# Chunk order of the last product pair, and where a norm adds its epsilon

## The chip, the cores and the metric

The kernel runs on one core of one Trainium2 chip. The metric is the device time of one execution in microseconds. The core has a matrix engine (TensorE, PE in the profile), three engines for elementwise work (VectorE, DVE; ScalarE, ACT; GpSimd, POOL) and SyncE (SP), which here only issues DMAs. GpSimd issues DMAs as well.

## The reference

Two layers of a hybrid of linear attention and chunked softmax attention, on 512 tokens of width 2048, in float32. Cut to what matters here:

```python
def hybrid_layer(x, ...):
    h = rmsnorm(x, g_pre)
    z = h @ w_in                       # one projection, split by columns
    gq, gk, gv, gg, ga, aq, ak, av, ag = split_columns(z)
    ...
    o_gla = gla_chunk_causal(...)      # 4 heads, value width 256
    o_gla = rmsnorm(o_gla, g_gla.reshape(GLA_HEADS, GLA_DV)).reshape(B, S, D_GLA)
    o_gla = o_gla * jax.nn.silu(gg)
    o_att = ...                        # 8 heads of softmax attention, normed and gated
    y = jnp.concatenate([o_gla, o_att], axis=-1) @ w_out
    return x + rmsnorm(y, g_post)
```

with `rmsnorm(x, g) = x * rsqrt(mean(x*x) + EPS) * g`, EPS = 1e-6.

## The kernel before

**Weights.** Each weight matrix is cut into blocks of 512 columns, and each block into eight pieces of 256 rows (512 KB each). A piece is a job in one long list, `stream`. A job is loaded by a DMA on SyncE into a ring of four tiles (`raw` or `H`), then split in two parts: ScalarE rounds it (`wh`, line 195), VectorE subtracts the rounded from the full (`wl`, line 199). TensorE multiplies three times: high by high, high by low, low by high. A loop keeps loads up to five jobs ahead of the products. When VectorE has read a `raw` tile for its low part, the tile is free for a later load.

**Pairs.** Most blocks are taken two at a time by `fast_gemm`, which multiplies a 2 by 2 arrangement of sub-matrices with seven products (P1 to P7) in place of eight. Each product runs over four chunks c = 0 to 3 of the inner dimension. The list `PROD` (for the last pair of a layer, `PROD_END`) gives the order of (product, chunk). The products P5, P6, P3 and P7 take sums of activation blocks as their operand (S1, S2, S4, S3). VectorE adds or subtracts the weight pieces for P5, P6, P7 and, in the last pair, P4 (lines 190 and 192). When a product's last chunk is done, its result is evacuated: P1, P5 and P6 by ScalarE copies, the others by VectorE (lines 357 to 361) and then a consumer, for the output projection `project` (square on ScalarE, line 1214, times a gain on VectorE, line 1217).

**The sums of the last pair.** The activations of the output projection are the gated heads. `output_sums` loads their four parts for a chunk (SyncE, lines 623 and 627, tiles `t`, from `fa` and `fg`), makes S1, S3, S2, S4 in turn on VectorE (lines 603 to 612), splits each (lines 108 and 109), and stores it to DRAM from GpSimd's queue (line 597, tensors `oS`). A job of P5 then loads its S1 back into a ring of four tiles named `sa` (line 180). The sums of chunks 2 and 3 (the attention heads 4 to 7 with the linear heads 2 and 3) are made while the value projection's products still run; those of chunks 0 and 1 only when all heads are done, during the block before the last pair. In program order a load of weights for P5 comes ahead of the load of its S1.

**The end of a layer.** Four blocks of the output projection: block 0 for all four token tiles, block 1 for the first two, the last pair (blocks 2 and 3, `W23`, with `end=True`), then block 1 for the other two token tiles. For the last block the attention operands of the second token half are loaded again by `fetch_last`, one with each chunk of P4, into `sa`. The table `OO` gives the order in which block 1 goes through its chunks.

**The linear heads.** A `Unit` is one head and one token half. Its steps: `outer` and `states` make the chunk states, `read` multiplies them with the queries (line 1071), `norm` squares the result on ScalarE with a sum along the row (line 1081, two calls), adds epsilon on VectorE (line 441, in `rms_scale`) and raises to the power of -0.5 on GpSimd (line 437); `gate` scales on VectorE (line 1089); `turn` transposes on TensorE (line 1099), evacuates on ScalarE (line 1110), splits, and stores to `fg`. There are four heads and two token halves, 8 units a layer and 16 in all. The operand tiles of the last two units are named `a` and `g` in the profile.

**Order.** All instructions are traced in the program's order, and the framework then plans each engine's order ahead of time on a simulated timeline (`schedule_with_timeline_sim=True`), so that an instruction which the plan thinks ready can go ahead of an earlier one that it thinks is waiting. On the chip the order of each engine and of each DMA queue is fixed.

Of the kernel before, what the change touches and what calls it, by code (L numbers as in the profile page):

```python
# [7 lines left out]
F32 = mybir.dt.float32  # L8
F32R = mybir.dt.float32r
BF16 = mybir.dt.bfloat16  # L10
AF = mybir.ActivationFunctionType
ALU = mybir.AluOpType
# [3 lines left out]
P = 128  # L16
# [9 lines left out]
EPS = 1e-6  # L26
# [8 lines left out]
def hybrid_trunk(  # L35
# [13 lines left out]
    nc = tc.nc  # L49
    cpool = ctx.enter_context(tc.tile_pool(name="cpool", bufs=1))  # L50
# [15 lines left out]
    def nm(s):  # L66
        serial[0] += 1
        return f"{s}_{serial[0]}"
# [10 lines left out]
    def ev():  # L79
        return tmp.tile([P, 512], F32, tag="ev", name=nm("ev"), bufs=6)  # L80
# [4 lines left out]
    def sm(cols, tag="sm", bufs=None):  # L85
        return small.tile([P, cols], F32, tag=tag, name=nm(tag), **({"bufs": bufs} if bufs else {}))

    def aux():
        return ps_ax.tile([P, 512], F32, tag="ax", name=nm("ax"))
# [30 lines left out]
    chunk_ind = cst[:, 2 * P : 2 * P + 2]  # L120
    ones = cst[:, 2 * P + 2 : 3 * P + 2]
    mhalf = cpool.tile([P, 4], F32, tag="mhalf", name="mhalf")
    later = cpool.tile([P, P], F32R, tag="later", name="later")

    CO = (0, 4, 1, 5, 2, 6, 3, 7)
    OO = (5, 4, 7, 6, 2, 3, 0, 1)
    PAIRS = ((GG0, GG1), (AV0, AV1), (QK01, QK23), (QK45, QK67), (GK, GQ), (GV0, GV1))
    W23 = (NB_IN + 2, NB_IN + 3)
    MIDDLE = [("P6", 0), ("P3", 0), ("P6", 1), ("P3", 1), ("P6", 2), ("P6", 3), ("P3", 2), ("P3", 3)]

    def products(*names):
        return [(p, c) for p in names for c in range(4)]

    PROD = products("P1", "P5") + MIDDLE + products("P7", "P2", "P4")
    PROD_END = products("P1", "P2", "P5") + MIDDLE + products("P7", "P4")
    LEFT = {"P5": "S1", "P6": "S2", "P3": "S4", "P7": "S3", "P4": "A22"}
    last_cast, last_load, last_low = [None], [None], [None]
    made = set()
# [68 lines left out]
    for l in range(L):  # L207
# [3 lines left out]
        for b0, b1 in PAIRS:  # L211
            pr = {}
            stream += [Job(l, k, c, b0, b1, pr) for k, c in PROD]
        for b in (NB_IN, NB_IN + 1):
            stream += [Job(l, "std", c, b) for c in OO]
        pr = {}
        stream += [Job(l, k, c, *W23, pr) for k, c in PROD_END]
        stream += [Job(l, "std", c, NB_IN + 1) for c in OO]
# [9 lines left out]
    def take(l, blk, kind, c):  # L228
        i = cursor[0]
        job = stream[i]  # L230
        assert (job.l, job.b0, job.kind, job.c) == (l, blk, kind, c)
        for what in ("load", "high", "low"):
            prepare(what, i + 1)
        cursor[0] += 1
        return job

    def ahead():
        i = cursor[0]
        for what, n in (("load", 3), ("high", 3), ("low", 3), ("load", 4), ("high", 4), ("load", 5)):
            prepare(what, i + n)  # L240
# [89 lines left out]
    def fast_gemm(l, pair, consume, rate=0.0, skip=0, feature_major=False, after=None, end=False, scaled=True):  # L330
        b0 = pair[0]
        acc = {n: [ps_mm.tile([P, W], F32, tag="mm", name=nm("mm")) for _ in range(2)] for n in roles[0]}
        roles.reverse()
        target = {"P1": "X", "P5": "Y", "P6": "X", "P3": "Y", "P7": "X", "P2": "Y", "P4": "X"}
        starts = ["P1", "P5", "P2"]
        if end:
            target.update(P2="Z", P4="Y")
            starts.append("P4")
        prod = PROD_END if end else PROD
        pace = Pace(rate, skip)  # L340
        keep = {}

        def copies(name, src):
            keep[name] = []
            for t in range(2):
                e = ev()
                if scaled:
                    nc.scalar.activation(e, src[t], AF.Copy, scale=inv_rms(l, 2 * (name == "p5") + t))
                else:
                    nc.scalar.copy(e, src[t])  # L350
                keep[name].append(e)

        def combine(ps, h, t, kept, sign, op):
            def f(dst):
                if scaled:
                    r = (inv_rms if sign > 0 else neg_inv_rms)(l, 2 * h + t)
                    nc.vector.scalar_tensor_tensor(out=dst, in0=ps, scalar=r, in1=kept, op0=ALU.mult, op1=op)
                elif sign > 0:
                    nc.vector.tensor_tensor(out=dst, in0=ps, in1=kept, op=op)
                else:  # L360
                    nc.vector.tensor_tensor(out=dst, in0=kept, in1=ps, op=ALU.subtract)
            return f

        def finished(k, t):
            x_, y_ = acc["X"][t], acc["Y"][t]
            if k == "P3":
                consume(1, 0, t, None, combine(y_, 0, t, keep["x"][t], 1, ALU.subtract))
            elif k == "P7":
                consume(1, 1, t, None, combine(x_, 1, t, keep["p5"][t], -1, ALU.add))
            elif k == "P2":  # L370
                consume(0, 0, t, None, combine(acc[target[k]][t], 0, t, keep["p1"][t], 1, ALU.add))
            elif k == "P4" and end:
                consume(0, 1, t, None, combine(y_, 1, t, keep["x"][t], 1, ALU.add))
            elif k == "P4":
                consume(0, 1, t, x_, None)

        def matmuls(job, k, c, ts):
            a = job.a if job.a is not None else A[{"P1": (0, 0, c), "P2": (1, 0, c), "P4": (1, 1, c)}[k]]
            out_ps = acc[target[k]]
            fresh = k in starts and c == 0  # L380
            for kk in range(2):
                if feature_major:
                    for ft in range(4):
                        f = slice(ft * P, (ft + 1) * P)
                        tok = slice(kk * 256, (kk + 1) * 256)
                        dst = out_ps[ft // 2][:, (ft % 2) * 256 : (ft % 2 + 1) * 256]
                        ops = ((job.wh, 0), (job.wh, 1), (job.wl, 0))
                        for m, (lhs, part) in enumerate(ops):
                            nc.tensor.matmul(  # L389
                                dst, lhs[:, kk, f], a[:, part, tok],  # L390
                                start=(fresh and kk == 0 and m == 0 and ft % 2 == 0),
                                stop=(c == 3 and kk == 1 and m == 2), skip_group_check=True,
                            )
                else:
                    for t in ts:
                        tok = slice(kk * 256 + t * P, kk * 256 + (t + 1) * P)
                        ops = ((0, job.wh), (0, job.wl), (1, job.wh))
                        for m, (part, rhs) in enumerate(ops):
                            nc.tensor.matmul(  # L399
                                out_ps[t], a[:, part, tok], rhs[:, kk, :],  # L400
                                start=(fresh and kk == 0 and m == 0),
                                stop=(c == 3 and kk == 1 and m == 2), skip_group_check=True,
                            )

        if end:
            acc["Z"] = None
        for k, c in prod:
            if k == "P2" and end and c == 0:
                acc["Z"] = [aux(), aux()]
            job = take(l, b0, k, c)  # L410
            matmuls(job, k, c, range(2))
            ahead()
            if c == 3:
                if k == "P1":
                    copies("p1", acc["X"])
                elif k == "P5":
                    copies("p5", acc["Y"])
                elif k == "P6":
                    copies("x", acc["X"])
                else:  # L420
                    for t in range(2):
                        finished(k, t)
                    if k == "P7" and end:
                        copies("x", acc["X"])
            if after is not None:
                after(k, c)
            pace()
# [10 lines left out]

    def rms_scale(out_r, ms):
        v = sm(ms.shape[-1])  # L440
        nc.vector.tensor_scalar(out=v, in0=ms, scalar1=EPS, scalar2=None, op0=ALU.add)
        rsqrt(out_r, v)

    def square_sum(out_ss, pieces):
# [53 lines left out]
    def inv_rms(l, t):  # L498
        return norm[l][:, 0, t : t + 1]
# [139 lines left out]
    for i in range(10):  # L639
        nc.tensor.matmul(ps_w, warm[:, 0:P], warm, start=True, stop=True)  # L640
    nc.gpsimd.memset(mhalf, -0.5)
    nc.vector.tensor_copy(later, cst[:, P : 2 * P])

    fg_weights = {}
# [27 lines left out]
    def layer(l):  # L672
# [106 lines left out]
        fresh = set()  # L779
# [496 lines left out]

        def fetch_last(k, c):
            if k == "P4":
                i = OO[c] - 4
                op_att[1, i] = rtile("sa", (2, 512), F32R)  # L1280
                nc.sync.dma_start(flat(op_att[1, i]), oa_d[l][1, i])

# [75 lines left out]
```

## Time and profile before

| what | us |
|---|---|
| three runs | 1666.9, 1667.8, 1672.28 (median 1667.8) |
| the profiled execution | 1665.86, its span 1664.1 |
| block 0, the linear heads and block 1 (636 to 726, layer 0): TensorE busy | 86.71 of 90 |
| P1, P2 and P5 of the last pair (726 to 756, layer 0) | 28.03 of 30 |
| the rest of the last pair (756 to 806, layer 0) | 49.88 of 50 |
| the same three in layer 1 (1462 to 1551, 1551 to 1584, 1584 to 1634) | 86.47 of 89, 29.09 of 33, 50.00 of 50 |
| the tail (1634 to 1664) | 21.71 of 30 |

A row of a timeline gives the start, the duration, the engine, the line, the operation, output<-input, shapes, how many instructions of that kind are merged into the row, and in brackets the idle time of the engine before it with what ended it. Rows of DMA instructions in a queue (SPq, POOL) show the time of the issue, not of the transfer. A row of the chain of waits gives start, duration and what the chain went through; there a DMA lasts from issue to landing. A row of a group (L..., xcount) ends with total busy us, mean ns of one, and idle time before them. A row of windows gives the stretch, its length, busy time of PE, PEld, DVE, ACT and POOL, the granted clock, the busy share of the DMA engines and GB/s. PE's matmuls overlap: one of 512 columns is shown as 0.39 us, but they start closer together.

### The profile page before, as it was taken

What the parts mean: (1) busy time and instruction counts of PE and PEld (TensorE: products, weight loads), DVE (VectorE), ACT (ScalarE), POOL (GpSimd) and SP (SyncE); (2) the same over time, 40 slices, a digit from 0 to 9 for tenths busy, and PEclk for the clock granted to TensorE, in tenths of its full rate; (3) what the DMA queues carried; (4) which work ended last, traced back from release to release, by engine and by line L of the source; (5) the groups of instructions that cost most, each with busy time, mean ns of one, the idle gap of its engine ahead of it and who ended that gap; (6) DMA issues with size and microseconds to landing.
All of it is one profiled execution on the core that took longest, in us unless ns stands there. A gap on an engine that the chain in (4) does not pass through costs nothing.

```text
span 1664.1 us, 24933 instructions
## 1 busy us (share of the span) xinstructions
PE 1634.7 (98%) x9030; PEld 1396.2 (84%) x9030; DVE 1226.4 (74%) x1595; ACT 901.4 (54%) x1499; POOL 166.5 (10%) x260
## 2 busy tenths in 40 slices
PE   9999999999999999999999999999999999999997
PEld 7888889999988877687888878899999888777776
DVE  7566776877876876678886676768778778856787
ACT  7444544565766544454784445445567665445443
POOL 1210000000100101310122000000010011013101
PEclk9999999999999999999999999999999999999999
DMA  9979786868867788798889687868587677878986
GB/s 378 343 269 321 282 305 232 301 188 301 280 193 271 276 322 265 272 337 302 292 290 399 221 331 258 312 224 297 193 312 249 223 275 287 298 240 302 347 291 234
DMA packets 150779, 470.64 MB, mean 283 GB/s; under 512 B 16428, under 2 KB 35636, under 8 KB 150656
## 3 DMA queue, kind: packets, MB, share of 16 engines
q1 hardware_dynamic: 127632, 389.36, 67.7%
q0 software_dynamic: 22304, 78.41, 12.3%
q8 instruction: 71, 1.16, 0.3%
q10 hardware_dynamic: 720, 1.28, 0.2%
q14 instruction: 52, 0.43, 0.1%
HBM read 396.88 MB, written 72.11 MB: 282 GB/s over the span
## 4 chain that ended last, share of the span: by engine, by line
PE 89%; DMA 6%; DVE 3%; issue 1%; ACT 1%; POOL 0%; DVEq 0%; SPq 0%; ACTq 0%; POOLq 0%
PE mm L399 41%; PE mm L314 19%; PE mm L389 18%; DMA raw<-in_w_dram 3%; PE ax L875 2%; DVE wl L199 1%; DMA t<-fg 1%; PE ax L858 1%; PE ax L1037 1%; PE ax L706 1%; DMA sa<-S 1%; PE ax L1071 1%; PE ax L836 1%; PE ax L838 1%; PE ax L837 1%
## 5 line engine op out<-in xcount | busy, mean ns | idle before, releaser
L399 PE MATMUL mm<-wh,sa 128*128 128x512 f32 x1536 | 487.7, 392 | 5.6 <-ACT wh L195 3.5
L195 ACT CAST wh<-raw 128x1024 fp32r<-128x1024 f32 x256 | 269.4, 1055 | 253.4 <-PE mm L399 84.7
L199 DVE TENSOR_TENSOR wl<-raw,wh 128x1024 fp32r<-128x1024 f32 x256 | 311.3, 1218 | 91.7 <-PE mm L314 30.9
L195 ACT CAST wh<-H 128x1024 fp32r<-128x1024 f32 x224 | 234.8, 1051 | 217.9 <-PE mm L399 122.3
L399 PEld LDWEIGHTS mm<-wh,sa 128*128 128x128 f32 x1536 | 288.6, 188 | 68.5 <-ACT wh L195 6.4
L199 DVE TENSOR_TENSOR wl<-H,wh 128x1024 fp32r<-128x1024 f32 x224 | 272.7, 1221 | 79.8 <-PE mm L399 29.8
L399 PE MATMUL mm<-wl,sa 128*128 128x512 f32 x768 | 301.5, 393 | 4.7 <-DVE wl L199 4.7
L389 PE MATMUL mm<-sa,wh 128*128 128x256 f32 x1280 | 238.1, 285 | 0.0
L389 PEld LDWEIGHTS mm<-sa,wh 128*128 128x128 f32 x1280 | 200.3, 191 | 0.5
L399 PE MATMUL mm<-wh,a 128*128 128x512 f32 x576 | 184.6, 392 | 0.0
L389 PE MATMUL mm<-sa,wl 128*128 128x256 f32 x640 | 181.3, 283 | 0.2 <-DVE wl L199 0.2
L399 PEld LDWEIGHTS mm<-wl,sa 128*128 128x128 f32 x768 | 144.6, 188 | 37.2 <-DVE wl L199 7.6
L314 PE MATMUL mm<-wh,a 128*128 128x512 f32 x512 | 172.3, 402 | 2.6 <-DVE g L1217 0.9
L190 DVE TENSOR_TENSOR H<-H,raw 128x1024 f32<-128x1024 f32 x120 | 145.7, 1220 | 11.2 <-DMA raw<-in_w_dram 9.5
L192 DVE TENSOR_TENSOR raw<-H,raw 128x1024 f32<-128x1024 f32 x56 | 68.6, 1225 | 82.4 <-DMA raw<-in_w_dram 82.2
L399 PEld LDWEIGHTS mm<-wh,a 128*128 128x128 f32 x576 | 108.0, 188 | 22.3
L437 POOL TENSOR_TENSOR sm<-sm,mhalf 128x4 f32<-128x4 f32 (+2 forms) x40 | 54.3, 1357 | 694.0 <-DVE sm L885 450.6
L389 PEld LDWEIGHTS mm<-sa,wl 128*128 128x128 f32 x640 | 122.4, 191 | 0.5 <-DVE wl L199 0.4
L314 PEld LDWEIGHTS mm<-wh,a 128*128 128x128 f32 x512 | 98.1, 192 | 26.1 <-DVE g L1217 1.8
L399 PE MATMUL mm<-wl,a 128*128 128x512 f32 x288 | 113.5, 394 | 0.0
L314 PE MATMUL mm<-wl,a 128*128 128x512 f32 x256 | 102.2, 399 | 0.0
L389 PE MATMUL mm<-a,wh 128*128 128x256 f32 x512 | 94.7, 284 | 0.0
(205 smaller groups left out, 2345.0 us busy)
## 6 DMA issues: line engine op xcount, KB each, us to landing
raw<-in_w_dram SPq DMA_DIRECT2D x320, 512.0 KB, 5.2
sa<-S SPq DMA_DIRECT2D x192, 512.0 KB, 4.8
H<-in_w_dram SPq DMA_DIRECT2D x56, 512.0 KB, 4.8
sa<-A SPq DMA_DIRECT2D x48, 512.0 KB, 5.5
S<-g POOLq DMA_DIRECT2D x32, 512.0 KB, 7.7
oS<-g POOLq DMA_DIRECT2D x32, 512.0 KB, 6.4
sa<-oS SPq DMA_DIRECT2D x32, 512.0 KB, 5.1
sg<-t POOLq DMA_DIRECT2D x32, 256.0 KB, 5.8
```

The source lines that it names most:

```text
L190: nc.vector.tensor_tensor(out=h, in0=h, in1=r, op=ALU.add)
L192: nc.vector.tensor_tensor(out=r, in0=h, in1=r, op=ALU.subtract)
L195: last_cast[0] = nc.scalar.copy(self.wh, src).ins
L199: last_low[0] = nc.vector.tensor_tensor(out=self.wl, in0=self.src, in1=self.wh.bitcast(F32), op=ALU.subtract).ins
L314: mm = nc.tensor.matmul(pss[o], a[:, part, t], rhs[:, kk, :], start=(i == 0 and kk == 0 and m == 0), stop=(i == n - 1 and kk == 1 and m == 2),
L389: nc.tensor.matmul(dst, lhs[:, kk, f], a[:, part, tok], start=(fresh and kk == 0 and m == 0 and ft % 2 == 0), stop=(c == 3 and kk == 1 and ...
L399: nc.tensor.matmul(out_ps[t], a[:, part, tok], rhs[:, kk, :], start=(fresh and kk == 0 and m == 0), stop=(c == 3 and kk == 1 and m == 2), ...
L437: nc.gpsimd.tensor_tensor(out=out_r, in0=v, in1=mhalf[:, : v.shape[-1]], op=ALU.pow)
L706: nc.tensor.matmul(ps[0:96, half * 256 : (half + 1) * 256], wga[kt // 10][:, kt % 10, :], op[:, i, (kt % 2) * 256 : (kt % 2 + 1) * 256], s ...
L836: nc.tensor.matmul(ps[:, :n], self.qh[:, t], self.kh[:, :n], start=True, stop=False)
L837: nc.tensor.matmul(ps[:, :n], self.qh[:, t], self.kl[:, :n], start=False, stop=False)
L875: nc.tensor.matmul(o, self.pt[i][:, j * P : (j + 1) * P], av[hd // 4, j // 2][:, j % 2, (hd % 4) * P : (hd % 4 + 1) * P], start=(j == 0), ...
```

## The change

Two parts. In the last pair of each layer every product takes its chunks in the order 2, 3, 0, 1: `C_END` replaces 0, 1, 2, 3 in `PROD_END`, the first and the last chunk of a product (which start and stop the accumulation, and set off the evacuation) follow it, and `fetch_last` looks its index up through it, so that the k-th chunk of P4 still fetches the k-th operand. In `rms_scale`, which only `norm` of the linear heads calls, the epsilon is added by ScalarE (Identity with a bias from a tile of one column, set once by GpSimd at the start) where VectorE added it.

```diff
+    eps = cpool.tile([P, 1], F32, tag="eps", name="eps")
...
-    MIDDLE = [("P6", 0), ("P3", 0), ("P6", 1), ("P3", 1), ("P6", 2), ("P6", 3), ("P3", 2), ("P3", 3)]
-
-    def products(*names):
-        return [(p, c) for p in names for c in range(4)]
-
-    PROD = products("P1", "P5") + MIDDLE + products("P7", "P2", "P4")
-    PROD_END = products("P1", "P2", "P5") + MIDDLE + products("P7", "P4")
+    C_IN, C_END = (0, 1, 2, 3), (2, 3, 0, 1)
+    MIDDLE = (("P6", 0), ("P3", 0), ("P6", 1), ("P3", 1), ("P6", 2), ("P6", 3), ("P3", 2), ("P3", 3))
+
+    def products(cs, *names):
+        return [(p, c) for p in names for c in cs]
+
+    def middle(cs):
+        return [(p, cs[i]) for p, i in MIDDLE]
+
+    PROD = products(C_IN, "P1", "P5") + middle(C_IN) + products(C_IN, "P7", "P2", "P4")
+    PROD_END = products(C_END, "P1", "P2", "P5")
+    PROD_END += middle(C_END) + products(C_END, "P7", "P4")
...
         prod = PROD_END if end else PROD
+        c_first, *_, c_last = C_END if end else C_IN
...
-            fresh = k in starts and c == 0
+            fresh = k in starts and c == c_first
...
-                                stop=(c == 3 and kk == 1 and m == 2), skip_group_check=True,
+                                stop=(c == c_last and kk == 1 and m == 2), skip_group_check=True,
...
-            if k == "P2" and end and c == 0:
+            if k == "P2" and end and c == c_first:
                 acc["Z"] = [aux(), aux()]
...
-            if c == 3:
+            if c == c_last:
...
     def rms_scale(out_r, ms):
         v = sm(ms.shape[-1])
-        nc.vector.tensor_scalar(out=v, in0=ms, scalar1=EPS, scalar2=None, op0=ALU.add)
+        nc.scalar.activation(v, ms, AF.Identity, bias=eps)
         rsqrt(out_r, v)
...
     nc.gpsimd.memset(mhalf, -0.5)
+    nc.gpsimd.memset(eps, EPS)
...
         def fetch_last(k, c):
             if k == "P4":
-                i = OO[c] - 4
+                i = OO[C_END.index(c)] - 4
```

More of the change, by code (lines that the diff above doesn't have):

```diff
@@ L401, in matmuls @@
                                 start=(fresh and kk == 0 and m == 0),
-                                stop=(c == 3 and kk == 1 and m == 2), skip_group_check=True,
+                                stop=(c == c_last and kk == 1 and m == 2), skip_group_check=True,
                             )
```

## The prediction

> **What bounds the kernel now.** I read the page first, then the list of waits of TensorE, then the timelines of the places that it names.
>
> ```profile
> span 1664.1 us, 24933 instructions
> ...
> PE 1634.7 (98%) x9030; PEld 1396.2 (84%) x9030; DVE 1226.4 (74%) x1595; ACT 901.4 (54%) x1499; POOL 166.5 (10%) x260
> ```
>
> TensorE is busy for 98% of the span: 29.4 us are left in which it does nothing, the start and the tail among them. No edit here takes a matmul away, so a gain can only come from those gaps, and from the slow matmuls behind some of them. The waits of TensorE say which gaps the change can touch:
>
> ```profile
> PE mm L399 <- DVE wl L199: 4.7, 6, 1.0
> PE ax L1099 <- issue: 3.7, 2, 1.9
> PE mm L399 <- ACT wh L195: 3.5, 3, 1.7
> ```
>
> L399 is the matmul of the paired products, L1099 the transposes that turn a gated head. Each kind of gap occurs once per layer: **the turn** of the last linear-attention head (near 695 us and 1521 us), and **product P5 of the last pair** (near 754 us and 1580 us). The timeline of TensorE at P5, layer 0 and then layer 1:
>
> ```profile
> 752.91 0.39 PE L399 MATMUL mm<-wh,sa 128*128 128x512 f32 x1
> ...
> 756.12 0.50 PE L399 MATMUL mm<-wl,sa 128*128 128x512 f32 x1 [0.98 <-DVE wl L199]
> ```
>
> ```profile
> 1575.37 0.39 PE L399 MATMUL mm<-wh,sa 128*128 128x512 f32 x1
> ...
> 1583.69 0.79 PE L399 MATMUL mm<-wl,sa 128*128 128x512 f32 x1 [0.99 <-DVE wl L199]
> ...
> 1587.28 1.32 PE L399 MATMUL mm<-wh,sa 128*128 128x512 f32 x5
> ```
>
> Matmuls without a wait start 0.23 us apart (the last row: five starts, 1.32 us less the 0.39 us that one lasts, over four steps). A product of one chunk is 12 matmuls, 2.7 us. In layer 0 the second row is the third start after the first: 3.21 us where 0.69 would do, **2.5 us lost**. In layer 1 it is the 15th: 8.32 us where 3.45 would do, **4.9 us lost**. Then come nine starts in 3.59 us (1583.69 to 1587.28) where 2.07 would do: 1.5 us more, at a lower pace although nothing is waited for. So P5 costs 2.5 us in layer 0 and 6.4 us in layer 1.
>
> What was late there? The chain of waits, layer 0 and layer 1:
>
> ```profile
> 736.73 9.73 DMA raw<-in_w_dram
> ...
> 750.05 0.69 DVE t L359
> ```
>
> ```profile
> 1563.19 10.86 DMA raw<-in_w_dram
> ...
> 1582.42 1.23 DVE wl L199
> ```
>
> The weights of P5's second chunk take 9.73 and 10.86 us to land. VectorE then adds them (L190), ScalarE rounds (L195), VectorE takes the low part (L199), and behind that, in VectorE's order, stand the evacuations of P2 (L359, L1217) and the add for the third chunk. Everything from the landing to the row at 1582.42 is a chain on VectorE that the late landing pushes.
>
> Why was it late? The queue of SyncE in layer 0, and the sizes:
>
> ```profile
> 721.72 0.70 SPq L627 DMA_DIRECT2D t<-fg  x1
> 725.04 0.33 SPq L180 DMA_DIRECT2D sa<-oS  x1
> 726.40 0.89 SPq L1204 DMA_DIRECT2D t<-in_g_post_dram  x2
> 734.30 0.33 SPq L147 DMA_DIRECT2D raw<-in_w_dram  x1
> 735.72 0.84 SPq L180 DMA_DIRECT2D sa<-oS  x2
> 736.73 0.49 SPq L147 DMA_DIRECT2D raw<-in_w_dram  x1
> 737.31 0.39 SPq L180 DMA_DIRECT2D sa<-oS  x1
> ```
>
> ```profile
> raw<-in_w_dram SPq DMA_DIRECT2D x320, 512.0 KB, 5.2
> ...
> sa<-oS SPq DMA_DIRECT2D x32, 512.0 KB, 5.1
> ```
>
> ```profile
> 726.00:756.00 30.00, 28.03 (x123) 22.57 (x121) 24.11 (x29) 14.78 (x23) 2.65 (x5) 1.00 0.94 352
> ```
>
> The last row is a window: DMA engines busy 0.94, 352 GB/s. The four `sa` loads are the operands S1 of chunks 0 to 3. Three of them leave between 735.72 and 737.31, around the second weight load at 736.73, whose median elsewhere is 5.2 us. They leave so late because S1 of chunk 1 must first be made and stored, and the queue is in order. GpSimd's stores of the sums:
>
> ```profile
> 697.75 0.54 POOL L597 DMA_DIRECT2D oS<-g  x1 [0.20 <-issue]
> ...
> 720.25 0.54 POOL L597 DMA_DIRECT2D oS<-g  x1 [17.22 <-DVE g L109]
> ...
> 732.80 0.53 POOL L597 DMA_DIRECT2D oS<-g  x1 [5.60 <-DVE g L109]
> ```
>
> The last of the eight sums of chunks 2 and 3 leaves at 697.75; S1 of chunk 0 leaves at 720.25, S1 of chunk 1 at 732.80.
>
> **The change, part one: chunks 2, 3, 0, 1.** The same matmuls, DMAs and bytes. What moves is the order of the loads: S1 of chunks 2 and 3 are first and wait for no store, so they can leave before 734.30. SyncE has nothing to send for 7.0 us there (727.29, the end of the row at 726.40, to 734.30), which covers them. Then of the three `sa` loads around the second weight load two are gone: 2 x 0.524 MB at 352 GB/s is **3.0 us** that the landing can come earlier. What speaks against the whole 3.0 us: the same 1.05 MB lie elsewhere in a nearly full stretch, and half of it may delay the loads that VectorE's sums wait for and so, in its order, the release of the weight buffers. I bound the advance by 0 and 3.0 us; with half the bytes in the hole and half in the way it is 1.5 at the least, and I take the middle of 1.5 and 3.0, **2.2 us**.
>
> In layer 0 VectorE's L359 (750.05) can't start before P2's last matmul, just before P5's first. P5's two chunks of 12 up to 752.91 start 5.3 us earlier, at 747.6, and that matmul ends about 0.2 us later. So an advance is worth 2.2 us at most: 2.2. In layer 1 the chain up to 1582.42 moves by the advance, and TensorE with it, since 2.2 is below the 4.9 lost: 2.2. What is late next is the same VectorE chain: 0.3 us remain in layer 0 and 2.7 in layer 1, so I leave the 1.5 us of slow matmuls where they are. Part one: **-4.4 us** (bounds 0 and -8.9, all of P5's loss).
>
> The reordered P4 loads (`fetch_last`) are mapped back through C_END, so the last block finds them in the order that it uses: 0.
>
> **Part two: epsilon on ScalarE.** It removes 16 VectorE instructions and adds 16 on ScalarE, one memset and a tile.
>
> ```profile
> L441 DVE TENSOR_SCALAR sm<-sm x16: 158/166/270, 625.5 to 1517.7; 128x2 f32<-128x2 f32 x16
> ```
>
> ```profile
> L881 ACT ACTIVATION_READ_ACCUMULATOR t<-ax 128x1 f32 x64 | 12.6, 197 | 0.0
> ...
> L840 ACT ACTIVATE t<-bias,norm 128x128 f32<-128x128 f32 x16 | 6.4, 398 | 0.0
> ```
>
> An Identity on 128x2 isn't in the trace. The nearest rows are 0.20 us (one column) and 0.40 us (128 columns with a scale from a tile); I take 0.2, near the smaller tile. The Trainium skill speaks against the move: in "ScalarE: Activation LUTs", Rules for kernel authors, adds belong on VectorE, and an activation with a bias from a tile is put at some 280 ns plus 0.83 ns per element, an estimate of 0.28 us; the sum would change by 0.1 us.
>
> The step's own 0.166 us matters less than its place: it waits in VectorE's order though ScalarE has long finished. Whether that is on the path shows at the turn, layer 0, ScalarE and then TensorE:
>
> ```profile
> 690.78 0.20 ACT L1081 ACTIVATION_READ_ACCUMULATOR t<-ax 128x1 f32 x1
> ...
> 694.69 0.83 ACT L1110 ACTIVATE t<-ax,gcol 128x256 f32<-128x256 f32 x2
> 695.55 0.62 ACT L108 CAST a<-t 128x512 fp32r<-128x512 f32 x1
> ```
>
> ```profile
> 689.50 0.50 PE L314 MATMUL mm<-wh,g 128*128 128x512 f32 x1 [0.46 <-ACT g L108]
> ...
> 693.02 0.60 PE L1099 MATMUL ax<-cst,bias 128*128 128x128 f32 x4
> 695.48 1.22 PE L1099 MATMUL ax<-cst,sg 128*128 128x128 f32 x4 [1.86 <-issue]
> 696.35 0.77 PE L314 MATMUL mm<-wh,a 128*128 128x512 f32 x1
> ```
>
> The squares of the last unit end at 690.98, its transposes start at 695.48: 4.5 us, of which the new chain could save one or two. But the matmul behind them, at 696.35, reads `a`, which ScalarE finishes at 696.17 (695.55 + 0.62), from the unit before. Were the second transposes early, TensorE would wait for that cast instead. So the gain is 0.2 us (696.35 - 696.17). Against it, ScalarE's 0.2 us stand ahead of a cast for which TensorE already waits (689.50), and perhaps 0.4. I take 0.1 us of loss per layer, **+0.2 us** for both. Bounds: -7.1 us, if the turn's gaps (3.7) and some 3.4 us of slow matmuls and the next short wait go, and +0.8 us (0.4 in each layer).
>
> **Sum:** -4.4 + 0.2 = -4.2 us. The profiled execution took 1665.86 us for its span of 1664.1; it would take 1661.7. The median of the runs shown is 1667.8, 1.9 us above it, so I forecast **1663.6 us**, 0.25% down.
>
> **The rivals.**
> *All gaps close.* Weights land the full 3.0 us earlier, the planner sets the third chunk's add ahead of P2's evacuations, and the earlier pow lets the unit before be gated and turned earlier too: 8.9 + 3.7 would be 12.6 us. For it: the same gaps come in both layers, and little else gives. Against: ScalarE's cast at the turn. Between 6 and 12.6, say 9: 1658.8 us.
> *Nothing moves.* DMA engines at 0.94 only shift the wait: the loads put forward delay those for the sums by the 3.0 us that they free later. 1667.8 us, give or take 2.
> *Slower: the early S1 loads hold up VectorE.* VectorE does the sums in order with the low parts of the weights. P2's first low part, and its first use:
>
> ```profile
> 733.02 1.22 DVE L199 TENSOR_TENSOR wl<-raw,wh 128x1024 fp32r<-128x1024 f32 x1
> ```
>
> ```profile
> 737.27 0.39 PE L399 MATMUL ax<-wl,a 128*128 128x512 f32 x1
> ```
>
> It is done at 734.24, 3.0 us ahead. If 1.05 MB go ahead of the `t` loads of both chunks (721.72 is the last), VectorE slips 3.0 us twice; beyond 3.0 us in all TensorE waits. At 6.0 it is 3.0 us per layer and no gain: 1673.8 us. For it: the full DMA window. Against: it takes a slip at both chunks.
> *The function isn't in the loaded table set.* Then each norm could load a table and load it back:
>
> ```profile
> L60 ACT ACT_TABLE_LOAD x4 | 5.1, 1283 | 0.8 <-PEq L1346 0.7
> ```
>
> 2.6 us on ScalarE ahead of each turn's casts, 5.1 us for the last turns of both layers, and no gain: 1673 us. The Trainium skill ("ScalarE: Activation LUTs", Table sets) has identity in every set; no run here shows it.
>
> **Chances.** Forecast 0.43 (gains of 2 to 6 us), all gaps 0.22, nothing 0.21, VectorE held up 0.11, table 0.03. A measurement can tell about 0.3% from no change, 5.0 us. Of the forecast's 0.43 some 0.12 lies beyond 5.0 us: faster 0.34, same 0.31 + 0.21 = 0.52, slower 0.14. The range 1657.5 to 1669.0 leaves out the two slower cases (0.14) and the far end of the first rival (0.05).
>
> **What would show it.** Part one right: in SyncE's queue two `sa` loads lie before the first P5 weight load, the second weight load lands in 7 to 8 us, and the gaps at L399 from L195 and L199 shrink by half. Wrong: a wait of VectorE for `t<-fg` above 3 us, or the same landing. Part two right: no L441 on VectorE, and TensorE at the turn still waits about 2 us, for ScalarE's cast. Wrong: no gap at L1099, or a fifth table load. The forecast fails if the planned order of the engines changes elsewhere.

## The result, and the profile after

The changed kernel takes 1658.07 us (median of 6 runs, 1656.54 to 1661.03) beside 1670.16 us for the kernel before (6 runs, 1666.9 to 1672.28): a ratio of **0.9932, 95% interval 0.9918 to 0.9946**, 0.7% faster. The profiled executions are 1665.86 us before and 1658.24 us after, 7.6 us apart. The time lies within the predicted range (1657.5 to 1669.0), 0.6 us above its lower end and 5.5 us below the forecast of 1663.6.

All line numbers after the change are larger: L399 is L406, L195 is L201, L199 is L205, L190 is L196, L359 is L366, L1099 is L1107. The page of the changed kernel, and the longest waits of its TensorE (total us, times, longest):

```profile
span 1656.5 us, 24943 instructions
...
PE 1629.2 (98%) x9030; PEld 1393.2 (84%) x9030; DVE 1224.4 (74%) x1579; ACT 905.0 (55%) x1515; POOL 162.8 (10%) x261
```

```profile
PE mm L406 <- DVE wl L205: 3.8, 5, 1.3
PE ax L1107 <- issue: 3.8, 2, 2.0
```

The wait of L399 for ScalarE's `wh` (3.5 us before) is off the list, and the wait at the turn is as long as it was. The waits that are left at L406 are elsewhere; P5 has none. The windows around P5 of the last pair, layer 0 and layer 1, of the kernel before and then of the changed kernel:

```profile
744.00:764.00 20.00, 17.92 (x78) 13.91 (x77) 16.29 (x17) 9.66 (x13) 0.00 (x0) 1.00 0.85 318
1565.00:1590.00 25.00, 21.09 (x83) 16.08 (x82) 18.80 (x19) 9.02 (x12) 0.19 (x1) 0.93 0.85 307
```

```profile
744.00:764.00 20.00, 20.00 (x90) 16.49 (x89) 18.39 (x18) 10.63 (x14) 0.00 (x0) 1.00 0.89 307
1565.00:1590.00 25.00, 25.00 (x111) 20.65 (x110) 22.38 (x22) 12.84 (x16) 0.00 (x0) 1.00 0.87 314
```

Before, TensorE is idle for 2.08 and 3.91 us there, and in layer 1 the granted clock is 0.93 of 25 us, some 1.75 us more: 7.7 us in all. After, it is idle for nothing, at full clock. That is about as much as the two profiled executions differ (7.6 us), but it is not the whole account. Both run 9030 matmuls; by the times of the matmuls with the same number, the changed kernel gains 2.9 us at P5 of layer 0 and 6.4 us at P5 of layer 1, together 9.3 us, and the rest of the execution takes 1.7 us of that back. (The windows see less: an idle stretch begins where a matmul is shown to end, 0.39 us after its start, though the next could start after 0.23.) The queue of SyncE in the changed kernel, both layers:

```profile
680.66 1.34 SPq L186 DMA_DIRECT2D sa<-oS  x1
...
695.64 0.33 SPq L186 DMA_DIRECT2D sa<-oS  x1
...
727.64 0.33 SPq L186 DMA_DIRECT2D sa<-oS  x1
...
733.39 2.67 SPq L153 DMA_DIRECT2D raw<-in_w_dram  x2
737.15 0.33 SPq L186 DMA_DIRECT2D sa<-oS  x1
...
1557.53 2.75 SPq L153 DMA_DIRECT2D raw<-in_w_dram  x2
```

The S1 loads of chunks 2 and 3 leave at 680.66 and 695.64, 47 and 32 us ahead of the stretch (from 727.29) for which they were predicted. No S1 load lies between the first two weight loads of P5. The second one leaves at about 735.7 in layer 0 (733.39 + 2.67, less the 0.33 us of one issue) and 1559.95 in layer 1. VectorE, the kernel before and then the changed one:

```profile
735.49 1.22 DVE L199 TENSOR_TENSOR wl<-raw,wh 128x1024 fp32r<-128x1024 f32 x1
...
746.48 1.22 DVE L190 TENSOR_TENSOR H<-H,raw 128x1024 f32<-128x1024 f32 x1 [2.96 <-DMA raw<-in_w_dram]
...
1561.94 1.22 DVE L199 TENSOR_TENSOR wl<-raw,wh 128x1024 fp32r<-128x1024 f32 x1
...
1574.07 1.23 DVE L190 TENSOR_TENSOR H<-H,raw 128x1024 f32<-128x1024 f32 x1 [4.36 <-DMA raw<-in_w_dram]
```

```profile
734.45 1.22 DVE L205 TENSOR_TENSOR wl<-raw,wh 128x1024 fp32r<-128x1024 f32 x1
...
743.75 1.22 DVE L196 TENSOR_TENSOR H<-H,raw 128x1024 f32<-128x1024 f32 x1
...
747.44 1.23 DVE L196 TENSOR_TENSOR H<-H,raw 128x1024 f32<-128x1024 f32 x1
748.58 0.69 DVE L366 TENSOR_TENSOR t<-ax,ev 128x512 f32<-128x512 f32 x1
...
1558.71 1.22 DVE L205 TENSOR_TENSOR wl<-raw,wh 128x1024 fp32r<-128x1024 f32 x1
...
1564.61 2.35 DVE L196 TENSOR_TENSOR H<-H,raw 128x1024 f32<-128x1024 f32 x2
...
1571.12 0.69 DVE L366 TENSOR_TENSOR t<-ax,ev 128x512 f32<-128x512 f32 x1 [0.97 <-PE ax L406]
1571.73 1.22 DVE L196 TENSOR_TENSOR H<-H,raw 128x1024 f32<-128x1024 f32 x1
```

Three things are to be seen. First, a weight load of P5 leaves when VectorE has read the tile that it takes over: before, 735.49 + 1.22 = 736.71 and the load is issued at 736.73; after, 735.67. Second, the add for the second chunk (746.48 before) waits 2.96 us for the landing, and after (743.75) not at all: the load lands in 8.0 us at most, in layer 1 in 5.8 at most (the second add of the row at 1564.61 starts about 1565.8), where it took 9.73 and 10.86. Third, in layer 0 the plan now has the third chunk's add (747.44) ahead of P2's evacuation (748.58). In layer 1 it does not go so far: the add (1571.73) stands behind P2's first evacuation (1571.12) and ahead of the second, where before both were ahead of it.

At the turn, layer 0, first ScalarE and then TensorE:

```profile
697.31 0.62 ACT L108 CAST a<-t 128x512 fp32r<-128x512 f32 x1
```

```profile
697.34 0.89 PE L1107 MATMUL ax<-cst,sg 128*128 128x128 f32 x4 [1.96 <-issue]
697.99 0.50 PE L320 MATMUL mm<-wh,a 128*128 128x512 f32 x1
```

The wait is 1.96 us (1.86 before), and the matmul behind it starts 0.06 us after the cast of `a` ends at 697.93. The new instruction, and the table loads:

```profile
L448 ACT ACTIVATE sm<-sm,eps x16: 288/299/330, 626.9 to 1516.7; 128x2 f32<-128x2 f32 x16
```

```profile
L60 ACT ACT_TABLE_LOAD x4 | 5.1, 1283 | 0.8 <-PEq L1354 0.7
```

### The profile page after: what moved, and what is told of

Its sections match the earlier page's. It is cut to its first block, busy times and chain, and to the rows that moved or that the text cites. A ratio compares the mean times of both kernels' runs of the same rounds, so it can differ in the third digit from the quotient of the medians.

```text
span 1656.5 us, 24943 instructions
## 1 busy us (share of the span) xinstructions
PE 1629.2 (98%) x9030; PEld 1393.2 (84%) x9030; DVE 1224.4 (74%) x1579; ACT 905.0 (55%) x1515; POOL 162.8 (10%) x261
## 4 chain that ended last, share of the span: by engine, by line
PE 93%; DMA 3%; DVE 2%; issue 1%; ACT 1%; POOL 0%; DVEq 0%; SPq 0%; ACTq 0%; POOLq 0%
PE mm L406 44%; PE mm L320 20%; PE mm L396 18%; PE ax L883 2%; PE ax L406 1%; DMA raw<-in_w_dram 1%; PE ax L866 1%; PE ax L1045 1%; DVE wl L205 1%; DMA t<-fg 1%; PE ax L714 1%; DMA sa<-S 1%; PE ax L1079 1%; PE ax L844 1%; PE ax L846 1%
## 5 line engine op out<-in xcount | busy, mean ns | idle before, releaser
L406 PE MATMUL mm<-wh,sa 128*128 128x512 f32 x1536 | 486.7, 392 | 2.2 <-DMA sa<-S 2.1
L201 ACT CAST wh<-raw 128x1024 fp32r<-128x1024 f32 x256 | 269.4, 1055 | 252.0 <-PE mm L406 81.6
L205 DVE TENSOR_TENSOR wl<-raw,wh 128x1024 fp32r<-128x1024 f32 x256 | 311.4, 1219 | 95.7 <-PE mm L320 34.3
L201 ACT CAST wh<-H 128x1024 fp32r<-128x1024 f32 x224 | 234.9, 1051 | 217.1 <-PE mm L406 118.5
L406 PEld LDWEIGHTS mm<-wh,sa 128*128 128x128 f32 x1536 | 288.2, 188 | 64.3 <-issue 2.7
L205 DVE TENSOR_TENSOR wl<-H,wh 128x1024 fp32r<-128x1024 f32 x224 | 273.0, 1221 | 81.8 <-PE mm L406 30.2
L406 PE MATMUL mm<-wl,sa 128*128 128x512 f32 x768 | 300.7, 392 | 3.5 <-DVE wl L205 3.5
L406 PE MATMUL mm<-wh,a 128*128 128x512 f32 x576 | 184.5, 392 | 0.0
L406 PEld LDWEIGHTS mm<-wl,sa 128*128 128x128 f32 x768 | 144.3, 188 | 34.9 <-DVE wl L205 5.2
L196 DVE TENSOR_TENSOR H<-H,raw 128x1024 f32<-128x1024 f32 x120 | 145.6, 1219 | 3.9 <-DMA raw<-in_w_dram 2.1
L406 PEld LDWEIGHTS mm<-wh,a 128*128 128x128 f32 x576 | 108.1, 188 | 22.2
L444 POOL TENSOR_TENSOR sm<-sm,mhalf 128x4 f32<-128x4 f32 (+2 forms) x40 | 50.7, 1267 | 688.7 <-DVE sm L893 451.4
L406 PE MATMUL mm<-wl,a 128*128 128x512 f32 x288 | 113.5, 394 | 0.0
```

Source lines behind the costliest of these rows:

```text
L196: nc.vector.tensor_tensor(out=h, in0=h, in1=r, op=ALU.add)
L201: last_cast[0] = nc.scalar.copy(self.wh, src).ins
L205: last_low[0] = nc.vector.tensor_tensor(out=self.wl, in0=self.src, in1=self.wh.bitcast(F32), op=ALU.subtract).ins
L406: nc.tensor.matmul(out_ps[t], a[:, part, tok], rhs[:, kk, :], start=(fresh and kk == 0 and m == 0), stop=(c == c_last and kk == 1 and m == ...
L444: nc.gpsimd.tensor_tensor(out=out_r, in0=v, in1=mhalf[:, : v.shape[-1]], op=ALU.pow)
```

## The experiments

All ratios are to runs of the kernel before on the same chip as the kernel beside it. "Idle at P5" is the length of the stretches 740 to 780 and 1555 to 1605 us less TensorE's busy time in them; the last column adds what a granted clock below 1.00 costs over 744 to 764 and 1565 to 1590 us (0.91 of 20 us is 1.8 us).

| kernel | ratio, 95% interval | idle at P5, layers 0 and 1, us | sum with the clock, us |
|---|---|---|---|
| before | 1 | 2.08, 3.91 | 7.7 |
| changed | 0.9932, 0.9918 to 0.9946 | 0, 0 | 0 |
| e1, order alone | 0.9936, 0.9924 to 0.9948 | 0.15, 0 | 0.2 |
| e2, epsilon alone | 0.9988, 0.9974 to 1.0003 | 3.08, 3.82 | 8.7 |
| e3, S1 loads held back | 0.9950, 0.9937 to 0.9963 | 0.89, 0.90 | 1.8 |
| e4, add first | 0.9986, 0.9976 to 0.9996 | 2.01, 1.76 | 5.6 |
| e7, old order, S1 loads held back | 0.9934, 0.9921 to 0.9948 | 1.24, 0.82 | 2.1 |
| e8, new order, two S1 loads ahead | 0.9961, 0.9948 to 0.9974 | 1.52, 3.10 | 4.6 |
| e6, turn earlier | 1.0032, 1.0021 to 1.0043 | 0.71, 0.32 | 1.0 |

### Each part alone: e1 and e2

e1 is the changed kernel with the epsilon back on VectorE:

```diff
-        nc.scalar.activation(v, ms, AF.Identity, bias=eps)
+        nc.vector.tensor_scalar(out=v, in0=ms, scalar1=EPS, scalar2=None, op0=ALU.add)
```

> Only the chunk order 2, 3, 0, 1; epsilon stays on VectorE. Theory O (the whole gain is the chunk order): the ratio to the kernel before is that of the full change, 0.992 to 0.994, and no gap of TensorE above 0.3 us is left at P5 in either layer. Rival E (a part of the gain is the epsilon: it ends the slow matmuls behind the last turn, 0.9 us in layer 0 and 1.5 us in layer 1 before): the ratio is 0.994 to 0.996, and matmuls behind the turn start 0.43 us apart again in both layers.

e2 is the changed kernel with the chunks back in their old order:

```diff
-    C_IN, C_END = (0, 1, 2, 3), (2, 3, 0, 1)
+    C_IN, C_END = (0, 1, 2, 3), (0, 1, 2, 3)
```

> Only the epsilon on ScalarE; chunks in the order 0, 1, 2, 3. Theory O: ratio 0.999 to 1.001; the gaps at P5 are those of before (2.5 us lost in layer 0, 4.9 us and slow matmuls in layer 1), and TensorE waits 1.8 to 2.0 us at the last turn for ScalarE's cast of the unit before. Rival E: ratio 0.996 to 0.998, with full pace behind both turns.

e1 gives the ratio of the whole change (0.9936) and no gap at P5 beyond 0.15 us; e2 gives 0.9988 with an interval that holds 1, and gaps like those of before (3.08 and 3.82 us). In e2's chain of waits the second weight load is as late as ever:

```profile
739.37 10.07 DMA raw<-in_w_dram
749.46 1.24 DVE H L196
```

The gain is the order of the chunks; the epsilon's part can't be told from nothing.

### Early S1 loads, or VectorE's order? e3 and e4

The new order does two things at P5: S1 loads leave early, and the plan moves the third add forward, in layer 0 ahead of both evacuations of P2. e3 keeps the changed kernel but ties each S1 load of P5 behind its own weight load, so that none is early:

```diff
-                nc.sync.dma_start(flat(self.a), src)
+                with tc.issue_after(last_load[0]) if end and k == "P5" else nullcontext():
+                    nc.sync.dma_start(flat(self.a), src)
```

> The full change, but on SyncE each S1 load of P5 is held behind its own weight load, so that the loads of chunks 2 and 3 leave at 733 us and later again, as before; in VectorE's planned order the add for P5's third chunk still stands ahead of the evacuations of P2. Theory L (the gain comes from the two loads that leave some 50 us earlier and so free the DMA engines around the second weight load): the second weight load takes 9 to 11 us to land again and most of the loss comes back, ratio 0.997 to 1.000. Rival V (the gain comes from VectorE's order, in which the add of the third chunk no longer waits behind the evacuations): ratio 0.992 to 0.995.

e4 has the old order of chunks (epsilon on ScalarE), with VectorE's order forced: P2's first evacuation behind the third add.

```diff
-            project(2 * h + t, 2 + j, settled(src, comb), gains[j])
+            with tc.issue_after(adds[-2]) if (j, h) == (0, 0) else nullcontext():
+                z = settled(src, comb)
+            project(2 * h + t, 2 + j, z, gains[j])
```

> Chunks in the order 0, 1, 2, 3 and epsilon on ScalarE, but VectorE's order is made that of the full change: the adds for P5's third and, here, fourth chunk stand ahead of the evacuations of P2. The S1 loads leave as late as before. Theory L: the second chunk's weights still land late, so the wait for the second chunk stays (0.9 us and 0.5 us in layer 1) and the third's shrinks a little: ratio 0.997 to 1.000. Rival V: no gap above 0.5 us at P5, ratio 0.992 to 0.995.

Neither theory holds in both runs. With the loads late (e3) most of the gain stays, 0.9950, as theory V had it; with the add first (e4) nearly none comes, 0.9986, as theory L had it. SyncE's queue at P5 of layer 0 in e3, and then in e4, shows what differs between them besides the order of the chunks:

```profile
735.91 0.33 SPq L153 DMA_DIRECT2D raw<-in_w_dram  x1
736.29 0.45 SPq L187 DMA_DIRECT2D sa<-oS  x1
738.33 0.33 SPq L153 DMA_DIRECT2D raw<-in_w_dram  x1
```

```profile
735.34 0.33 SPq L153 DMA_DIRECT2D raw<-in_w_dram  x1
736.76 0.86 SPq L186 DMA_DIRECT2D sa<-oS  x2
737.76 0.40 SPq L153 DMA_DIRECT2D raw<-in_w_dram  x1
```

In e4, as before the change, two S1 loads go between the first and the second weight load; in e3 one does. In e4 the second add starts at 747.11 after a wait of 2.83 us for its landing, 9.35 us after the issue. In e4's layer 1 the framework's order is another: one S1 load between the first and the second weight load, two between the second and the third. There the second add starts 7.26 us after the issue (1563.52 to 1570.78) and the third 10.96 us after (1565.89 to 1576.85): the delay has moved with the S1 loads. That gave the next theory: what counts is what is queued between the weight loads.

### The queue without the order, and the order without the queue: e7 and e8

e7 is the kernel before, chunks 0, 1, 2, 3 and epsilon on VectorE, with e3's edit alone.

> The kernel before (chunks in the order 0, 1, 2, 3, epsilon on VectorE) with one thing added: each S1 load of P5 in the last pair stands in SyncE's queue right behind its own chunk's weight load, as in e3_sa_behind, so that only one S1 load, and no longer that of chunk 1 and that of chunk 2, is ahead of the second weight load. Theory Q (what counts is what stands ahead of the second weight load in SyncE's queue; the order of the chunks only happens to move it): the ratio is that of e3_sa_behind, 0.993 to 0.997, the second add's DMA wait falls from 2.3 to 3 us to about 0.9 us, and at most one gap of TensorE over 0.3 us is left in P5 of layer 0. Theory M (the order of the chunks counts itself, because the stores of chunks 2 and 3 are done sooner): 0.998 to 1.001, the gaps at P5 stay as in the kernel before, and SyncE waits with the S1 load of chunk 1 ahead of the third weight load.

e8 is the changed kernel with its queue put back: the S1 loads of its second and third chunk go between the first two weight loads (their data were stored long before, so that no store holds the queue), the last one behind a weight load.

```diff
+                with tc.issue_after(s1_load[0]) if end and c == C_END[1] else nullcontext():
                     p["r", c] = self.fetch(rtile("raw"), b1, top)
...
+            if end and k == "P5" and c == C_END[0]:
+                for cc in C_END[1:3]:
...
+                    with tc.issue_after(last_load[0]):
+                        s1_load[0] = nc.sync.dma_start(flat(s1_tile[cc]), so_d[self.l]["S1", cc]).ins
```

> The changed kernel (order 2, 3, 0, 1, epsilon on ScalarE) with SyncE's queue at P5 of the last pair put back to that of the kernel before: the first S1 load free, then the first weight load, the second and third S1 loads, the second weight load. The data of these S1 loads are stored long before, so no store holds the queue, only 2 x 0.524 MB. VectorE's order has the third add ahead of P2's evacuation, as in the changed kernel. Theory Q-bytes (1.05 MB at the 352 GB/s of the profile before are 3.0 us on the second weight load): second weight load about 3 us later than in the changed kernel, TensorE gaps of together 2 to 5 us per layer at P5, ratio to the kernel before 0.996 to 1.000. Theory M (order of the chunks itself) and theory Q-store (only the wait for chunk 1's store, at the queue's head, counts): gaps of under 0.5 us per layer, ratio 0.992 to 0.995.

e7 gives 0.9934: **the whole ratio of the change, with the chunks in their old order.** VectorE in e7 and then in e8, where the second chunk's add waits for its weights:

```profile
744.55 1.22 DVE L191 TENSOR_TENSOR H<-H,raw 128x1024 f32<-128x1024 f32 x1 [0.94 <-DMA raw<-in_w_dram]
...
750.66 1.23 DVE L191 TENSOR_TENSOR H<-H,raw 128x1024 f32<-128x1024 f32 x1 [2.46 <-DMA raw<-in_w_dram]
```

```profile
749.42 1.23 DVE L207 TENSOR_TENSOR H<-H,raw 128x1024 f32<-128x1024 f32 x1 [2.71 <-DMA raw<-in_w_dram]
...
1573.42 1.22 DVE L207 TENSOR_TENSOR H<-H,raw 128x1024 f32<-128x1024 f32 x1 [3.25 <-DMA raw<-in_w_dram]
```

The first row of e7 is the second chunk's add; the row at 750.66 is the third chunk's. SyncE issues the second chunk's weights at 738.48 in e7, so they land in about 6.1 us (7.2 in layer 1, where the add waits 1.91 us). In e8 (740.68 and 1563.82) they take 8.7 and 9.6, and gaps of together 4.6 us come back. From issue to add it is 8.7 to 10.9 us wherever two S1 loads are between (both layers of before, of e2 and of e8, and e4's layer 0) and 5.8 to 7.3 with one (both layers of e7 and of e3, and e4's layer 1), without an exception. e3's layer 1 is one of them: its second weight load leaves at 1559.86, and the add starts 6.9 us later.

```profile
1566.79 1.22 DVE L197 TENSOR_TENSOR H<-H,raw 128x1024 f32<-128x1024 f32 x1 [2.02 <-DMA raw<-in_w_dram]
```

e8 brings back about 60% of the lost time at P5 (4.6 of 7.7 us) and of the ratio some 0.003 of 0.007. The ratio is at the near end of what the theory Q-bytes gave (0.996 to 1.000), and layer 0's gap of 1.52 us lies below its 2 to 5 us. So 2 x 0.524 MB ahead of the second weight load explain about half. What makes up the rest isn't settled: e8's first S1 load still leaves 40 us early, and its third add is still planned ahead of the evacuation (752.99, ahead of L377). In e7 and e3, too, the plan puts the third add first, so the queue was never tried with the old order on VectorE. The nearest to it is layer 1 of the changed kernel, where one evacuation stands ahead of the third add and P5 has no gap all the same. By e4 VectorE's order alone takes P5's loss to 5.6 us, with no effect that the runs can tell from e2's.

In e7 and e3 the S1 loads aren't early, only behind. The third chunk's weights are then the late ones (the row at 750.66 waits 2.46 us; over 744 to 760 us the busy share of the DMA engines is 1.02 in e7, at 408 GB/s), and 1.8 to 2.1 us of gaps are left. In the changed kernel, where two of them are long done, none is.

### Does the rest belong to the kernel? Second profiles

Behind the turns the granted clock was 0.91 over 20 us before, in both layers, and 1.00 after, which looked like 3.6 us of gain. The kernel before, the changed one and e7 were profiled again, unchanged, all three on one chip, another than those of the experiments.

> The kernel before, profiled a second time, unchanged. Open is whether the stretches behind the turns, where the granted clock is 0.91 over 690 to 710 us and 1515 to 1535 us in the profile before and 1.00 in that of the changed kernel, belong to the kernel or to the one execution. Theory K (they belong to the kernel's order): 0.91 in both again, and TensorE's idle time at P5 is 2.1 us (744 to 764 us) and 3.9 us (1565 to 1590 us) again. Theory X (they come and go): at least one of the two stretches is at 1.00; the P5 gaps are as before all the same.

> The changed kernel, profiled a second time, unchanged. Theory K: 1.00 behind both turns, no TensorE idle time at P5 in either layer. Theory X: 0.91 behind one turn or both, and still no idle time over 0.3 us at P5.

> e7_sa_behind_0123, profiled a second time, unchanged: in its first profile 1.00 behind the first turn, 0.91 behind the second, and 1.2 and 0.8 us of TensorE idle at P5. Theory K: the same again. Theory X: the clock behind the turns changes, the idle time at P5 stays within 0.5 us.

The windows of the turns and of P5, the second profile of the kernel before and then of the changed one:

```profile
690.00:710.00 20.00, 16.31 (x71) 12.54 (x72) 12.24 (x21) 11.09 (x25) 8.67 (x14) 1.00 0.93 321
744.00:764.00 20.00, 16.96 (x66) 12.90 (x65) 15.31 (x17) 7.73 (x11) 0.00 (x0) 0.91 0.84 317
...
1515.00:1535.00 20.00, 17.14 (x78) 12.60 (x78) 13.99 (x24) 12.35 (x29) 9.20 (x14) 1.00 0.95 348
1565.00:1590.00 25.00, 21.96 (x89) 17.14 (x88) 20.14 (x21) 11.29 (x16) 1.07 (x2) 0.93 0.89 328
```

```profile
690.00:710.00 20.00, 17.58 (x69) 13.40 (x70) 11.27 (x17) 10.68 (x23) 7.97 (x12) 0.91 0.97 357
744.00:764.00 20.00, 20.00 (x90) 16.54 (x89) 18.18 (x18) 10.64 (x14) 0.00 (x0) 1.00 0.87 314
...
1515.00:1535.00 20.00, 17.92 (x74) 13.99 (x73) 11.29 (x16) 10.50 (x20) 6.11 (x10) 0.91 0.95 345
```

The clock behind the turns has changed sides: now it is 1.00 before the change and 0.91 after it. It comes and goes; none of the gain is to be put down to it. P5 stays: 3.04 + 3.04 us idle and some 3.6 us of clock before, 9.6 us in all, and nothing after. Of these the gaps are steady (6.0 us the first time, 6.1 the second), and the clock behind them varies (1.75 and 3.6). The second executions took 1666.97 and 1656.99 us, 10.0 apart. So twice the difference of the executions is about P5's loss, 7.7 for 7.6 and 9.6 for 10.0. Matmul for matmul P5 gains 5.6 and 5.2 us in this pair, 10.8 us, and the rest of the execution takes 0.8 us back. e7's second profile has 1.31 and 0.48 us at P5 (1.24 and 0.82 the first time).

### The gap at the turn: e6

With P5 closed the turn's two waits of 1.8 to 2.0 us are the largest that are left. e6 is the changed kernel with the turn put 3 steps after the gate.

```diff
-                delayed.append([5, units[k].turn])
+                delayed.append([3, units[k].turn])
```

> The changed kernel with the turn of the linear attention's units put off by 3 steps of the weave, not 5, so that its instructions stand earlier in every engine's order. If the turn's wait of 1.8 to 2.0 us per layer is a matter of where it stands, the two gaps close and the ratio to the kernel before is 0.990 to 0.992 (about 1655 us); if ScalarE's casts are late anyway, the gap stays and it is 0.993 to 0.995; if the earlier turn waits for products that are not there yet, it is slower than the changed kernel, 0.995 to 1.005.

It is slower, 1.0032. TensorE near the turn of layer 0 in e6:

```profile
696.72 0.50 PE L320 MATMUL mm<-wh,g 128*128 128x512 f32 x1 [3.84 <-ACT g L108]
...
702.82 0.94 PE L1107 MATMUL ax<-cst,bias 128*128 128x128 f32 x4 [1.48 <-DVE bias L1097]
...
705.92 0.80 PE L320 MATMUL mm<-wh,a 128*128 128x512 f32 x1 [2.16 <-ACT a L108]
```

The longest wait, 3.84 us, is for ScalarE's cast of `g`; near its turn the changed kernel waits 0.44 us for such a cast. The transposes now stand before the gate's result (1.48 us), the matmul behind them waits for ScalarE's cast of `a` all the same (2.16 us), and the granted clock over 690 to 710 us is 0.77. The third case of the expectations is what came. That the cast of `a` also sets the end of the turn in the changed kernel isn't shown beyond the 0.06 us above.

## Why the prediction was right in kind and short in size

**What bounds the kernel: right.** The gain that the profiles show came from P5 of the last pair, in both layers: its gaps and the slow matmuls behind them, which the prediction put at 2.5 + 6.4 us, are gone (2.9 and 6.4 us, matmul for matmul).

**Why the weights are late: right, and shown by e7.** The S1 loads around the second weight load delay it. The landing was expected to fall to 7 to 8 us; it is 6.1 and 7.2 in e7, at most 8.0 and 5.8 in the changed kernel. The size of 3.0 us came out too (9.35 in e4's layer 0 to 6.1 in e7's is 3.3), but not for its reason: the sum took two S1 loads away, and in e7 there is only one fewer between the weight loads, whose 0.524 MB would take 1.5 us at 352 GB/s. Why one load costs twice that stays open.

**The step that failed is the size of part one**: "What is late next is the same VectorE chain: 0.3 us remain in layer 0 and 2.7 in layer 1, so I leave the 1.5 us of slow matmuls where they are." Nothing remains. The term was -4.4 us; the two pairs of profiles give -7.7 and -9.6 by the windows, -9.3 and -10.8 matmul for matmul. Three things were missed. The advance of 2.2 us assumed that the early loads go in SyncE's 7 us hole, half of their bytes in the way; they left 47 and 32 us ahead of it, and no sum of VectorE waited longer for its own loads. VectorE's low parts of P2's weights, which free the tiles, are done earlier too, so the second load itself leaves earlier (736.73 to 735.7 and 1563.19 to 1559.95; about 1.3 us of the latter is TensorE's whole lead). And the VectorE chain was taken in its old order, though the plan made with the changed loads moves the third add ahead of both evacuations in layer 0 and of one in layer 1. The first rival named that reordering and the closing of all of P5's loss (8.9 us); with 9 us of gain it was the better forecast, for its part in P5 and not for the turn.

**Luck in the number.** Forecast and range were built on 1667.8 us, the median of three runs of the kernel before; the six runs beside the changed kernel have 1670.16. Of 1667.8 us the measured ratio would make 1656.5, just below the range. So that the time falls into the range owes something to a base that came out 2.4 us higher, and the nearness of the rival's 1658.8 us to 1658.07 is luck of the same kind.

**Part two: right.** Forecast +0.2 us; e2's interval holds no change and e1 without it is as fast. The instruction takes 0.30 us where 0.2 was taken, within the bounds. TensorE at the turn still waits 1.96 and 1.81 us, and its next matmul follows the cast of `a`. For the instruction the Trainium skill ("ScalarE: Activation LUTs", What ACT_TABLE_LOAD costs) gives some 280 ns plus 0.83 ns per element, an estimate of 0.28 us, which is nearer to the measured median of 0.299.

**The other rivals.** *Nothing moves* fell with the ratio. *VectorE held up* fell: no sum waits longer than before for its `t` loads; the last such wait in layer 1 is 0.42 us at L610 where it was 1.48 at L603. *The table set* fell: L60 still loads four times.

**What stays open.** The measured ratio is 11.4 us of 1670.16, the profiled executions are 7.6 and 10.0 us apart. The medians of the timed runs of the kernel before (1669.18 to 1670.47) lie some 2 to 5 us above its two profiled executions (1665.86 and 1666.97), that of the changed kernel does not (1658.07 beside 1658.24 and 1656.99), and no profile shows where.

## What to carry to other kernels

When a needed load is late, look at what is queued ahead of it and move that behind it: an ordering edit of one line (e7) was worth as much as the reordered computation. Work out an advance to the end of its chain, and ask whether a plan made ahead of time will reorder the engine behind it; where two gaps have one cause, the case in which both close belongs in the middle of the forecast. A lower clock seen once behind a gap is no property of the kernel until a second profile has it.

## What the runs showed of the hardware

The slow stretch behind a short wait comes and goes. At the turns TensorE's longest single wait is 1.81 to 2.04 us, with shorter ones beside it, and behind it the granted clock was 0.91 over 20 us in 9 of 22 stretches (both layers of before, changed, e1 to e4, e7, e8 and the three second profiles). The same kernel had it in both layers once and in neither the other time. The Trainium skill ("TensorE: Matmul & The Clock Gate", HAM oscillation) warns of idle gaps beyond some 3.4 us; here such a stretch stood at times behind waits of which none was longer than 2.04 us. The same page of the Trainium skill (What's actually happening) calls the window over which the clock's gate watches the engine free-running; that the slow stretch varies between executions of one kernel agrees with it.

Loads queued ahead on one queue have a price. With two S1 loads of 512 KB issued between two weight loads of the same size, the second weight load took 8.7 to 10.9 us from issue to use in nine cases; with one between, 5.8 to 7.3 us in seven (two profiles each of the kernel before and of e7, one of e2, e3, e4 and e8).
